# Channel shuffle: larger tiles, and each tile's copy halved over two engines

## The chip, the cores and the metric

The kernel runs on one core of a Trainium2 chip; the chip's other cores run nothing of it. The metric is the device time of one execution in microseconds (us). The *span* of a profile is the traced part of one execution; it is some 2 us shorter than the device time.

## The reference

The input has 256 float32 channels for each of 16 x 64 x 64 = 65,536 pixels. The channels are read as 8 groups of 32, and the two indices are swapped. Nothing is computed: 67.1 MB come in and 67.1 MB go out, in another order inside each pixel's 1 KB.

```python
x = x.reshape(batch, h, w, groups, channels_per_group)   # 16, 64, 64, 8, 32
x = x.transpose(0, 1, 2, 4, 3)
x = x.reshape(batch, h, w, c)
```

## The kernel before

A tile is 128 partitions x 16 pixels (16 KB a partition, 2 MB in all), and there are 32 of them. SyncE issues the loads, ScalarE issues the stores, and the swap of indices is one copy with a strided read. The copies go to GpSimd and VectorE in turn. There are five buffers for loaded tiles and five for tiles to be stored.

```python
_Q = 16; _IN_BUFS = 5; _OUT_BUFS = 5; _COPY_ENGINES = "gv"     # (shortened)
# ... pools in_pool and out_pool with that many buffers ...
for t in range(ntiles):                                        # 32
    in_tile = in_pool.tile([P, free], mybir.dt.float32)
    nc.sync.dma_start(out=in_tile, in_=x_t[t])
    out_tile = out_pool.tile([P, free], mybir.dt.float32)
    src = in_tile.rearrange("p (i g j) -> p i j g", g=G, j=CPG)
    dst = out_tile.rearrange("p (i j g) -> p i j g", j=CPG, g=G)
    do_copy(copy_engines[t % len(copy_engines)], dst, src)
    nc.scalar.dma_start(out=out_t[t], in_=out_tile)
```

## Time and profile before

| | before |
|---|---|
| device time, median | 318.0 us (317.92 to 318.02) |
| span of the profile | 316.3 us |
| VectorE / GpSimd busy | 20% / 36% of the span |
| DMA rate from 40 to 280 us | 431 GB/s, read plus written |

These lines are from the page of the kernel before. The row "DMA" gives the busy share of the 16 DMA engines in 40 equal slices of the span, in tenths; the row "GB/s" gives what they moved. The two lines that begin with L61 are the groups of copies: busy time and mean ns of one, then the idle time before them and what ended it.

```profile
span 316.3 us, 247 instructions
...
DMA  7999999999999999999999999999999999999997
GB/s 290 431 402 431 431 431 431 431 431 433 431 431 431 431 431 431 431 431 431 431 431 431 431 431 431 431 431 431 431 431 431 431 431 431 431 431 431 433 431 332
DMA packets 9216, 134.22 MB, mean 424 GB/s; under 512 B 1024, under 2 KB 1024, under 8 KB 1024
...
DMA 94%; DVE 1%; SPq 0%; issue 0%; DVEq 0%
DMA in_tile<-in_x_dram 94%; DVE out_tile L61 1%; SPq L65 0%; DVEq L61 0%
...
L61 POOL COPY out_tile<-in_tile 128x4096 f32<-128x4096 f32 x16 | 114.5, 7157 | 182.3 <-DMA in_tile<-in_x_dram 182.3
L61 DVE COPY out_tile<-in_tile 128x4096 f32<-128x4096 f32 x16 | 63.8, 3985 | 240.0 <-DMA in_tile<-in_x_dram 240.0
```

The DMA row is 9 nearly everywhere and the rate hardly moves. Both copy engines spend most of their time waiting for loads. The chain of waits, the two lines with 94% and 94%, consists of loads. In the trace's packet records, a data packet is one partition's row: 8,192 packets of 16,384 bytes, and 1,024 packets of 4 bytes that report completions to semaphores. Divided over the 16 DMA engines, that is 512 data packets and 64 semaphore packets each.

The table by stretches of the same trace (start:end in us, length, busy us of each engine with the number of instructions, TensorE's clock, DMA share, GB/s) shows where DMA is not saturated: only in the first and the last few us.

```profile
core 0: us, DVE busy (x) POOL busy (x), PEclk, DMA share, GB/s
0.00:40.00 40.00, 9.66 (x2) 18.02 (x7) 1.00 0.96 397
40.00:280.00 240.00, 46.34 (x12) 89.59 (x13) 1.00 1.01 431
280.00:312.00 32.00, 7.76 (x2) 7.11 (x1) 1.00 1.01 431
312.00:316.27 4.27, 0.00 (x0) 0.00 (x0) 1.00 0.58 249
```

Here 1.01 is no error of rounding. More than 16 packet records are open at times, so on one DMA engine the record of a packet must begin a little before the record of the packet before it ends.

### The profile page before, as it was taken

Reading aid. Unit: us, or ns where it says so; the run is one execution under the profiler, and the core shown is the slowest. Engines: PE = TensorE matmul, PEld = TensorE weight load, DVE = VectorE, ACT = ScalarE, POOL = GpSimd, SP = SyncE. Lnnn points to the kernel's source line nnn. Section 1 sums busy time; section 2 is a strip of 40 time slices with the busy share of each in tenths; the row PEclk is TensorE's granted clock in tenths of the full one; section 3 lists DMA queues with packets and bytes.
Section 4 is the critical chain, followed back from the end, with each engine's and each line's share of the span. In section 5 each row is a group of like instructions: output and inputs, shape, how many; then the busy total and the mean of one; then the engine's idle time right before and its main releaser. Section 6 shows DMA issues by size and latency. Waiting matters only on the chain.

```text
span 316.3 us, 247 instructions
## 1 busy us (share of the span) xinstructions
DVE 63.8 (20%) x16; POOL 114.7 (36%) x20
## 2 busy tenths in 40 slices
DVE  0344004040130402204021040310404004040040
POOL 0863350803508044080530806217062260713500
DMA  7999999999999999999999999999999999999997
GB/s 290 431 402 431 431 431 431 431 431 433 431 431 431 431 431 431 431 431 431 431 431 431 431 431 431 431 431 431 431 431 431 431 431 431 431 431 431 433 431 332
DMA packets 9216, 134.22 MB, mean 424 GB/s; under 512 B 1024, under 2 KB 1024, under 8 KB 1024
## 3 DMA queue, kind: packets, MB, share of 16 engines
q1 hardware_dynamic: 4608, 67.11, 50.0%
q10 hardware_dynamic: 4608, 67.11, 49.5%
HBM read 67.11 MB, written 67.11 MB: 424 GB/s over the span
## 4 chain that ended last, share of the span: by engine, by line
DMA 94%; DVE 1%; SPq 0%; issue 0%; DVEq 0%
DMA in_tile<-in_x_dram 94%; DVE out_tile L61 1%; SPq L65 0%; DVEq L61 0%
## 5 line engine op out<-in xcount | busy, mean ns | idle before, releaser
L61 POOL COPY out_tile<-in_tile 128x4096 f32<-128x4096 f32 x16 | 114.5, 7157 | 182.3 <-DMA in_tile<-in_x_dram 182.3
L61 DVE COPY out_tile<-in_tile 128x4096 f32<-128x4096 f32 x16 | 63.8, 3985 | 240.0 <-DMA in_tile<-in_x_dram 240.0
L90 POOL MEMSET const-float32-0.0<- 128x1 f32 x1 | 0.1, 99 | 0.2 <-issue 0.2
L90 POOL MEMSET const-bfloat16-1.0<- 128x1 bf16 x1 | 0.1, 103 | 0.0
L90 POOL MEMSET const-uint8-127<- 128x1 uint8 x1 | 0.1, 103 | 0.0
L90 POOL MEMSET const-float32-1.0<- 128x1 f32 x1 | 0.1, 99 | 0.0
## 6 DMA issues: line engine op xcount, KB each, us to landing
in_tile<-in_x_dram SPq DMA_DIRECT2D x32, 2048.0 KB, 38.8
out_dram<-out_tile ACTq DMA_DIRECT2D x32, 2048.0 KB, 25.3
```

The lines of the kernel that those rows point to most:

```text
L61: eng.tensor_copy(out=dst, in_=src)
L90: nc = _bacc.Bacc("TRN2", target_bir_lowering=False, num_devices=1)
```

## The change

Its intent is to move the same bytes in fewer, larger transfers, with the copy shortened by splitting each tile between VectorE and ScalarE, which leaves GpSimd free. There are 21 tiles of 24 KB a partition (3 MB) and a last one of 8 KB a partition, so that the last copy and store are short.

```diff
-_Q = 16
-_IN_BUFS = 5
-_OUT_BUFS = 5
-_COPY_ENGINES = "gv"
+_SIZES = [24] * 21 + [8]
+_IN_BUFS = 4
+_OUT_BUFS = 4
+_SHARES = (("vector", 1), ("scalar", 1))
 ... (row addressing for unequal tiles left out)
-    for t in range(ntiles):
-        ...
-        do_copy(copy_engines[t % len(copy_engines)], dst, src)
-        nc.scalar.dma_start(out=out_t[t], in_=out_tile)
+    for q in _SIZES:
+        in_tile = in_pool.tile([P, biggest * c], F32, name="in_tile")
+        nc.sync.dma_start(out=in_tile[:, : q * c], in_=rows(x_flat, first, q))
+        out_tile = out_pool.tile([P, biggest * c], F32, name="out_tile")
+        ... (for each engine of _SHARES, its columns:)
+                permute(engine, out_tile[:, cols], in_tile[:, cols])
+        nc.scalar.dma_start(out=rows(out_flat, first, q), in_=out_tile[:, : q * c])
+        first += P * q
```

More of the change, by code (lines that the diff above doesn't have):

```diff
@@ L2 @@
-import os
 from contextlib import ExitStack
@@ L8 @@
 from concourse._compat import with_exitstack
-_Q = int(os.environ.get("CS_Q", "16"))
-_IN_BUFS = int(os.environ.get("CS_IN_BUFS", "5"))
-_OUT_BUFS = int(os.environ.get("CS_OUT_BUFS", "5"))
-_COPY_ENGINES = os.environ.get("CS_COPY_ENGINES", "gv")
+F32 = mybir.dt.float32
+P = 128
+_SIZES = [24] * 21 + [8]
+_IN_BUFS = 4
+_OUT_BUFS = 4
+_SHARES = (("vector", 1), ("scalar", 1))
 @with_exitstack
@@ L29 @@
     CPG = c // G
-    assert G * CPG == c, (c, G)
-    P = nc.NUM_PARTITIONS
-    n_pix = b * h * w
-    assert n_pix % P == 0
-    q = _Q
-    pix_per_tile = P * q
-    ntiles = n_pix // pix_per_tile
-    assert ntiles * pix_per_tile == n_pix, (n_pix, pix_per_tile)
-    free = q * c
-    x_t = x.rearrange("b h w c -> (b h w c)").rearrange(
-        "(t p f) -> t p f", p=P, f=free
-    )
-    out_t = out.rearrange("b h w c -> (b h w c)").rearrange(
-        "(t p f) -> t p f", p=P, f=free
-    )
+    assert G * CPG == c
@@ L51 @@
+    assert sum(_SIZES) * P == b * h * w
+    biggest = max(_SIZES)
+    x_flat = x.rearrange("b h w c -> (b h w c)")
+    out_flat = out.rearrange("b h w c -> (b h w c)")
     in_pool = ctx.enter_context(tc.tile_pool(name="in_pool", bufs=_IN_BUFS))
     out_pool = ctx.enter_context(tc.tile_pool(name="out_pool", bufs=_OUT_BUFS))
-    eng_map = {"v": nc.vector, "g": nc.gpsimd, "s": nc.scalar}
-    copy_engines = [eng_map[ch] for ch in _COPY_ENGINES]
-    def do_copy(eng, dst, src):
-        if eng is nc.scalar:
-            eng.copy(out=dst, in_=src)
-        else:
-            eng.tensor_copy(out=dst, in_=src)
@@ L63, with rows @@
-    for t in range(ntiles):
-        in_tile = in_pool.tile([P, free], mybir.dt.float32)
-        nc.sync.dma_start(out=in_tile, in_=x_t[t])
-        out_tile = out_pool.tile([P, free], mybir.dt.float32)
-        src = in_tile.rearrange("p (i g j) -> p i j g", g=G, j=CPG)
-        dst = out_tile.rearrange("p (i j g) -> p i j g", j=CPG, g=G)
-        do_copy(copy_engines[t % len(copy_engines)], dst, src)
-        nc.scalar.dma_start(out=out_t[t], in_=out_tile)
+    def rows(flat, first, q):
+        return flat[first * c : (first + P * q) * c].rearrange("(p f) -> p f", p=P)
@@ new lines, in permute @@
+    def permute(engine, dst, src):
+        src = src.rearrange("p (i g j) -> p i j g", g=G, j=CPG)
+        dst = dst.rearrange("p (i j g) -> p i j g", j=CPG, g=G)
+        if engine == "scalar":
+            nc.scalar.copy(out=dst, in_=src)
+        else:
+            getattr(nc, engine).tensor_copy(out=dst, in_=src)
+    first = 0
+    for q in _SIZES:
+        in_tile = in_pool.tile([P, biggest * c], F32, name="in_tile")
+        nc.sync.dma_start(out=in_tile[:, : q * c], in_=rows(x_flat, first, q))
+        out_tile = out_pool.tile([P, biggest * c], F32, name="out_tile")
+        at, total = 0, sum(n for _, n in _SHARES)
+        for k, (engine, n) in enumerate(_SHARES):
+            last = k == len(_SHARES) - 1
+            upto = q if last else min(q, at + -(-q * n // total))
+            if upto > at:
+                cols = slice(at * c, upto * c)
+                permute(engine, out_tile[:, cols], in_tile[:, cols])
+            at = upto
+        nc.scalar.dma_start(out=rows(out_flat, first, q), in_=out_tile[:, : q * c])
+        first += P * q
```

## The prediction

> **What bounds the kernel now.** The 16 DMA engines, from end to end. The page's 40 slices show the DMA row at 9 (90% or more) in 38 of 40 and 431 GB/s in nearly all; the table by stretches gives a DMA share of 1.01 and 431 GB/s over 40 to 280 us. The queue table adds up to 99.5% of the span. VectorE is busy 20%, GpSimd 36%; both only wait for loads (240.0 and 182.3 us in the groups). The chain of waits is 94% DMA loads. In the trace's packet records nearly all 8192 data packets are 16384 bytes and last 611 ns; each of the 1024 semaphore packets lasts 9 ns. Per DMA engine that is 512 x 0.611 + 64 x 0.009 = 313.4 us: the whole span of 316.3 us less about 1.8 us before the first packet and 1.2 us after the last. The Trainium skill (DMA: Bandwidth & Descriptors, "Where 436 GB/s comes from") puts the fabric ceiling at 435.2 GB/s; the trace runs at 99% of it.
>
> **What the change does not touch.** The bytes: 67.1 MB in and 67.1 MB out.
>
> **What it changes, costed.**
> - The copy. A half tile is 3072 elements a partition: VectorE 3072/4096 x 3.87 us = 2.9 us (estimate from the steady copies). No ScalarE copy is in this trace; I guess 2.5 to 5 us. Both run at once, per tile period of 6.29 MB / 431 GB/s = 14.6 us, so neither engine comes near to binding. GpSimd's 114.7 us vanish. On the critical path: nothing.
> - Load depth. In the trace a load is issued when the fourth load before it lands (38.8 us to landing = four periods of 9.7 us). Afterwards it also waits for the copy out of its buffer: about 4 x 14.6 - 3 = 55 us to landing. The load queue stays full; stores also stay queued (about 25 us to landing). No starvation.
> - The start. The first load lands at about 10.9 us, not 8.5, but 12 MB of loads are queued by then, so DMA stays busy. The store backlog at the end (last load lands near 300 us, some 14 us of stores remain) hides the last copy as before; the small last tile therefore buys nothing.
> - Packets. 24 KB in place of 16 KB: 352 data and 44 semaphore packets per DMA engine in place of 512 and 64. Semaphores save 20 x 9 ns = 0.2 us. If a data packet has a fixed cost (611 ns against 602 ns at the ceiling of 435.2 GB/s leaves at most 9 ns; the same page, "Why small descriptors are slow", tells of a small fixed cost per packet), 160 fewer save up to 1.4 us. The trace cannot tell a fixed cost from a proportional one, so I take about half: 0.6 us.
>
> **Prediction.** 318.0 - 0.8 = 317.2 us, range 316.2 to 318.3. Chances: faster by over 2% 0.01, within 2% 0.98, slower by over 2% 0.01.
>
> **What would show each step right or wrong.** DMA row still at 9 and some 431 to 433 GB/s from start to end; 24 KB packets at 912 ns (fixed cost) or 916 ns (proportional); ScalarE and VectorE each under 40% busy, waiting for loads; the chain still over 90% DMA; loads about 55 us to landing; span about 315.5 us.
>
> **What would make it wrong.** Slices where the DMA share falls below 0.9: loads waiting for buffers with the queue empty, or stores held up on ScalarE's queue behind a copy that waits for a load. A ScalarE copy over 14 us, which would bind. Or the larger packets running at another rate, higher or lower, for a reason that the records of before don't show.

## The result

The time after is 317.73 us (317.58 to 317.88, 4 runs), against 318.01 us (317.92 to 318.13, 4 runs) for the kernel before. The ratio is 0.999, with a 95% interval from 0.9976 to 1.0005: the same. Ratios here are the mean time of one kernel's fast runs over that of the other's fast runs in the same rounds, so they are not quite the ratios of the medians quoted. Executions over 1.5% slower than the fastest of the same kernel are left out of the means.

The page of the kernel after, the lines that answer to those shown of before:

```profile
span 316.0 us, 236 instructions
...
DMA  8999999999999999999999999999999999999996
GB/s 302 439 395 426 426 445 432 420 442 439 417 439 445 417 436 442 426 426 445 426 423 445 439 414 442 442 417 439 442 421 432 442 420 432 442 429 429 421 446 291
DMA packets 6337, 134.23 MB, mean 425 GB/s; under 512 B 704, under 2 KB 704, under 8 KB 704
...
another core or an unknown queue 43%; DMA 32%; ACT 20%; ACTq 1%; issue 0%
DMA in_tile<-in_x_dram 32%; ACT out_tile L49 20%; ACTq L66 1%; ACTq L49 0%
...
L49 ACT COPY out_tile<-in_tile 128x3072 f32<-128x3072 f32 (+1 forms) x22 | 117.7, 5348 | 184.6 <-DMA in_tile<-in_x_dram 184.6
L51 DVE COPY out_tile<-in_tile 128x3072 f32<-128x3072 f32 (+1 forms) x22 | 65.3, 2968 | 238.3 <-DMA in_tile<-in_x_dram 238.3
...
in_tile<-in_x_dram SPq DMA_DIRECT2D x21, 3072.0 KB, 52.6
out_dram<-out_tile ACTq DMA_DIRECT2D x21, 3072.0 KB, 20.2
```

And the table by stretches of the kernel after:

```profile
40.00:280.00 240.00, 50.22 (x17) 89.29 (x17) 0.00 (x0) 1.00 1.00 432
280.00:312.00 32.00, 5.41 (x3) 10.89 (x3) 0.00 (x0) 1.00 0.99 426
312.00:315.97 3.97, 0.00 (x0) 0.00 (x0) 0.00 (x0) 1.00 0.44 188
```

The DMA row is as full as before. The rate in the middle stretch is 432 in place of 431 GB/s. The groups' mean mixes the small tile in; the groups kept apart by shape give 5.51 us for ScalarE's half of a 24 KB tile and 3.06 us for VectorE's. Both engines still wait for loads.

The chain of waits looks quite different: loads fell from 94% to 32%, ScalarE's copy appears with 20%, and 43% has no known releaser. That is no new bottleneck. With four buffers a load is issued when the copy frees its buffer, no longer when an earlier load lands. The waits of SyncE's queue show it; first before, then after:

```profile
SPq L65 <- DMA in_tile<-in_x_dram: 244.1, 27, 10.0
```

```profile
SPq L56 <- DVE out_tile L51: 184.6, 17, 12.0
...
SPq L56 <- ACT out_tile L49: 39.7, 17, 2.6
```

So the walk back from the last instruction now steps from load to copy to load. But the DMA engines had other loads and stores queued all the while, as the DMA row shows, and the time hardly changed. Two of the experiments below fit this, and show that the turn doesn't come from the halved copy: e4, the fastest kernel, copies in the old way with three buffers and has 34% loads in its chain; e2, with the halved copy and five buffers, has 87%.

One more thing is seen in the trace, and it matters in the experiments. ScalarE copies its halves and also issues the stores, one instruction after the other. From the third tile on its instructions come in the order copy, copy, store, store, although the kernel's text writes a store after each copy. So every second store stands behind the next tile's copy, and that copy waits for its load:

```profile
292.64 5.43 ACT L49 COPY out_tile<-in_tile 128x3072 f32<-128x3072 f32 x1 [9.11 <-DMA in_tile<-in_x_dram]
302.35 1.94 ACT L49 COPY out_tile<-in_tile 128x1024 f32<-128x1024 f32 x1 [4.29 <-DMA in_tile<-in_x_dram]
302.41 2.25 ACTq L66 DMA_DIRECT2D out_dram<-out_tile  x2
```

The tile copied from 292.64 us was ready at 298.07, but its store was issued at 302.41, just after the last copy had begun (the line with x2 merges this issue with that of the last tile). In all, 10 of the 22 stores of after were held in this way, for up to 9.3 us; in before, every store was issued within 0.03 us of its copy. With four buffers the DMA engines had enough other work: at 302.4 us, about 0.9 MB of earlier stores was still unfinished.

### The profile page after: what moved, and what is told of

It reads as the page before. It is cut to its first block, busy times and chain, and to the rows that moved or that the text cites. A ratio compares the mean times of both kernels' runs of the same rounds, so it can differ in the third digit from the quotient of the medians.

```text
span 316.0 us, 236 instructions
## 1 busy us (share of the span) xinstructions
DVE 65.3 (21%) x22; ACT 118.9 (38%) x23; POOL 0.2 (0%) x4
## 4 chain that ended last, share of the span: by engine, by line
another core or an unknown queue 43%; DMA 32%; ACT 20%; ACTq 1%; issue 0%
DMA in_tile<-in_x_dram 32%; ACT out_tile L49 20%; ACTq L66 1%; ACTq L49 0%
## 5 line engine op out<-in xcount | busy, mean ns | idle before, releaser
L49 ACT COPY out_tile<-in_tile 128x3072 f32<-128x3072 f32 (+1 forms) x22 | 117.7, 5348 | 184.6 <-DMA in_tile<-in_x_dram 184.6
L51 DVE COPY out_tile<-in_tile 128x3072 f32<-128x3072 f32 (+1 forms) x22 | 65.3, 2968 | 238.3 <-DMA in_tile<-in_x_dram 238.3
## 6 DMA issues: line engine op xcount, KB each, us to landing
in_tile<-in_x_dram SPq DMA_DIRECT2D x21, 3072.0 KB, 52.6
out_dram<-out_tile ACTq DMA_DIRECT2D x21, 3072.0 KB, 20.2
```

The lines of the kernel that those rows point to most:

```text
L49: nc.scalar.copy(out=dst, in_=src)
L51: getattr(nc, engine).tensor_copy(out=dst, in_=src)
```

## Where the gain in the steady part went

From the packet records one can work out three terms of a span. The first is the time that all 134.2 MB would take at the rate measured from 40 to 280 us. The second is what the start costs beyond that: 40 us less the time that the bytes moved up to 40 us need at that rate. The third is the same for the end, from 280 us on. They add up to the span. (One trace each; the sizes are KB a partition.)

| kernel | span, us | all bytes at the steady rate | lost at the start | lost at the end |
|---|---|---|---|---|
| before, 16 KB | 316.3 | 311.2 | 3.5 | 1.6 |
| after, 24 KB | 316.0 | 310.3 | 3.5 | 2.1 |

The change gained 0.87 us in the steady part, and lost 0.56 us at the end. The span is 0.3 us shorter, as is the time. Differences of some tenths between single traces need care: the spans of before scatter from 316.0 to 316.5 us. But the steady term repeats. It is 311.2 and 311.3 us in e1 and e2 below, which have 16 KB too, and 310.3 us in e8 and e12, which have 24 KB.

The steady part obeys a simple sum. From the number of packets served between 40 and 280 us, one can compute the time from one data packet to the next on one DMA engine: 607.8 ns for 16 KB and 909.1 ns for 24 KB, the semaphore packets included. The Trainium skill (DMA: Bandwidth & Descriptors, "Where 436 GB/s comes from") gives a ceiling of 435.2 GB/s, which is 27.2 bytes per ns for one of 16 engines. At that rate 16,384 bytes take 602.4 ns and 24,576 bytes take 903.5 ns. In both cases about 5.5 ns remain. A fixed cost of about 5.5 ns a packet was thus the theory to be tested (called F below). The records' own lengths, 611 and 912 ns, would give about 9 ns (called R), but they overlap, as the DMA share of 1.01 shows.

## The experiments

Runs e1 to e4, e5 to e8, e9 to e11, and e12 were four groups on three chips; each group shared its runs of the kernel before, which gave medians of 318.08, 318.05, 318.05 and 317.99 us.

### e1: no copy at all

```diff
-_IN_BUFS = 5
+_IN_BUFS = 10
-        do_copy(copy_engines[t % len(copy_engines)], dst, src)
-        nc.scalar.dma_start(out=out_t[t], in_=out_tile)
+        nc.scalar.dma_start(out=out_t[t], in_=in_tile)
```

> The kernel before without any copy (ten buffers of one pool, each tile stored as it was loaded; the result is wrong on purpose). Theory T1, the DMA engines bind from end to end and the copies are hidden: 318.0 us, as before, within 0.4. Rival T2, the copies or the engines they run on cost part of the time: at least 1 us under before.

It measured 318.69 us (318.46 to 318.92, 5 runs), ratio 1.0022 (1.0008 to 1.0036). Its output is wrong, which doesn't matter for the time. Taking away every copy saves nothing, so T2 falls. Nor do the copies slow the packets: their pace was 607.8 ns here as well. It is even 0.6 us slower, more than the 0.4 us that T1 allowed; its profiled span was 316.3 us, like that of before. Device time less span was 2.1 us in all five executions, against 1.8 us in before, so about half of the 0.6 us lies outside the profiled span. The cause stays open.

### e2: the halved copy alone

```diff
-_SIZES = [24] * 21 + [8]
-_IN_BUFS = 4
-_OUT_BUFS = 4
+_SIZES = [16] * 32
+_IN_BUFS = 5
+_OUT_BUFS = 5
```

> The new code with the old tile size and buffer counts (32 tiles of 16 KB a partition, five buffers): only the halved copy on VectorE and ScalarE changes. T1: 318.0 us within 0.3, so none of the 0.3 us gain belongs to the copy. T2, the gain comes from the copy: 317.7 us as after.

It measured 319.0 us (318.78 to 319.41, 5 runs), ratio 1.0031 (1.0019 to 1.0044). Neither number was met. The gain does not come from the halved copy, which cost about 0.9 us here. Its span was 317.0 us: 311.3 at the steady rate, 3.5 at the start, 2.2 at the end. So 0.6 of the 0.7 us lost in the span lies at the end, where 1.69 us passed after the last packet in place of 1.17 us. Nearly all of that is in one place: SyncE's first drain instruction after its last wait began 0.4 us later than in before, and took 0.12 us longer. Why is not known.

### e3, e4 and e5: other row lengths, the old copies

```diff
-_Q = 16;  _IN_BUFS = 5;   _OUT_BUFS = 5
+_Q = 8;   _IN_BUFS = 10;  _OUT_BUFS = 10      # e3
+_Q = 32;  _IN_BUFS = 3;   _OUT_BUFS = 3       # e4
+_Q = 4;   _IN_BUFS = 20;  _OUT_BUFS = 20      # e5
```

> The kernel before with 8 KB a partition (64 tiles, ten buffers): twice the packets. From the two traces, a 16 KB packet occupies its DMA engine for 607.8 ns from one to the next and a 24 KB one for 909.1 ns, so about 5.5 ns beyond the line rate, a fixed cost that includes the semaphore packets. Theory F with this cost: 512 more packets per engine x 5.5 ns = +2.8 us, 320.8 us. Rival R, the length of the packet records (9 ns a packet and 9 ns a semaphore packet): +5.0 us, 323.0 us. Rival P, no fixed cost: 318.0 us.

> The kernel before with 32 KB a partition (16 tiles, three buffers each): half the packets, whole-tile copies still on GpSimd and VectorE in turn. F: 256 fewer packets per engine x 5.5 ns = -1.4 us, 316.6 us. R: -2.5 us, 315.5 us. P: 318.0 us.

> The kernel before with 4 KB a partition (128 tiles, twenty buffers): four times the packets. F (5.5 ns a packet): 1536 more packets per engine, +8.4 us, 326.4 us. R (9 ns a packet and 9 ns a semaphore packet): +15.0 us, 333 us. P: 318.0 us.

| KB a partition | measured, us (range, runs) | ratio | F said | R said |
|---|---|---|---|---|
| 4 (e5) | 328.02 (327.76 to 328.29, 6) | 1.0315 | 326.4 | 333 |
| 8 (e3) | 322.12 (321.72 to 322.62, 4) | 1.0129 | 320.8 | 323.0 |
| 32 (e4) | 316.67 (316.52 to 317.10, 5) | 0.9961 | 316.6 | 315.5 |

P, no effect of the packets, falls. F meets 32 KB, and is 1.3 and 1.6 us short at 8 and 4 KB. The three terms say why:

| kernel | span, us | all bytes at the steady rate | lost at the start | lost at the end |
|---|---|---|---|---|
| e5, 4 KB | 326.2 | 319.9 | 3.6 | 2.7 |
| e3, 8 KB | 320.8 | 314.1 | 3.5 | 3.2 |
| e4, 32 KB | 315.3 | 309.8 | 3.7 | 1.7 |

In the steady part F holds for all: +8.7 us at 4 KB (8.4 expected), +2.9 at 8 KB (2.8), -1.4 at 32 KB (-1.4). From one packet to the next it is 156.2, 306.8 and 1210.1 ns, that is 5.6, 5.6 and 5.4 ns more than the bytes need at 27.2 bytes per ns. The page's ceiling is not even needed: a straight line through the five paces (4 to 32 KB) has a slope of 27.2 bytes per ns and leaves 5.6 ns, and no pace is off it by more than 0.11 ns. What these runs cannot tell is to what the fixed cost belongs. In each of them a transfer is eight data packets and one semaphore packet on each engine, so 5.5 ns a packet and some 44 ns a transfer would look alike. The rest is lost at the end, and differs from kernel to kernel by up to 1.6 us. The steady stretches of 4, 8 and 32 KB, in that order:

```profile
40.00:280.00 240.00, 52.60 (x48) 92.08 (x48) 1.00 1.03 420
```

```profile
40.00:280.00 240.00, 48.70 (x24) 89.85 (x25) 1.00 1.01 427
```

```profile
40.00:280.00 240.00, 45.13 (x6) 92.10 (x7) 1.00 1.00 433
```

The DMA share, the second-last figure of a line, falls from 1.03 to 1.00 while the rate rises from 420 to 433 GB/s. The more packets there are, the more records overlap. A DMA share of 1 does not mean that there is nothing to gain.

### e8: the small tile first

```diff
-_SIZES = [24] * 21 + [8]
+_SIZES = [8] + [24] * 21
```

> The new kernel with its small tile first instead of last. If the last copy is hidden under the stores still queued, the small last tile buys nothing: 317.7 us within 0.3. Rival, it shortens the tail: at least 1 us slower than after, since the last copy is then 5.4 us instead of 1.9 and the last store 3 MB instead of 1 MB.

It measured 317.34 us (317.27 to 317.70, 4 runs), ratio 0.9980 (0.9967 to 0.9994). That is 0.06 us below the range named for the first theory. The rival falls: with a full 24 KB tile last, nothing is lost. By the three terms, 3.5 us were lost at the start and 1.9 us at the end, no more than in after. The medians say 0.4 us faster than after, but the two intervals of the ratios overlap, so no more is claimed than that the small last tile buys nothing.

### e6 and e7: two buffers each

```diff
-_IN_BUFS = 4
-_OUT_BUFS = 4
+_IN_BUFS = 2
+_OUT_BUFS = 2
```

In e7 the sizes are `[48] * 10 + [32]` as well.

> The new kernel with two buffers for loads and two for stores in place of four. If a queue of DMA work never runs dry because loads and stores back each other up: 317.7 us within 0.5. Rival, the depth of four is needed: over 320 us, with slices where the DMA share falls below 0.9.

> The new kernel with tiles of 48 KB a partition (ten, and a last one of 32 KB), two buffers each: 176 packets per engine in place of 352. F: 176 x 5.5 ns = 1.0 us under after, 316.7 us, if nothing is lost at the ends. R: -1.7 us, 316.0 us. If the larger tiles lose at the start and at the end what they save per packet, as after seems to have done (0.87 us saved in the steady part, 0.3 us in the span): 317.7 us or more.

Both missed by far. e6 measured 325.9, 330.9 and four times 334.4 to 335.3 us. The profiled execution was the fastest, so the others count as slow ones beside it and there is no ratio; on one core this says only that its times scatter. e7 measured 335.91 us (335.86 to 336.83, 4 runs), ratio 1.0569. The halved number of packets was worth nothing beside what two buffers cost.

Stretches of e7: the early part, a later part, and a gap near the end.

```profile
40.00:130.00 90.00, 11.56 (x3) 26.78 (x3) 0.00 (x0) 1.00 1.00 375
140.00:200.00 60.00, 8.48 (x3) 18.29 (x3) 0.00 (x0) 1.00 1.00 432
302.00:308.00 6.00, 0.51 (x1) 0.55 (x1) 0.00 (x0) 1.00 0.13 57
```

Two different losses are seen. From 302 to 308 us the DMA engines were nearly idle (0.13): the last load had landed, and the last copy waited for a store to land and free its buffer. But there was work to do. The tile before the last, 6.3 MB, had been copied by 298.74 us; its store stood behind that last copy in ScalarE's order and was issued at 307.53 us. From 40 to 130 us, on the other hand, the DMA engines were busy throughout, at 375 GB/s in place of 432. There the packets themselves took longer: on average 43 ns per KB on the loads' queue and 44 on the stores' queue, in place of 37.8. What made them slow, and what ended it near 135 us, is not known. Of e6 only the fastest execution has a trace. It shows a weaker effect of the kind with 24 KB rows: from 40 to 280 us, at 428 GB/s, its load packets took 38.8 ns per KB, against 38.0 in after, and its store packets 38.0. So 48 KB rows are not needed for some slowing. Whether they made it larger, and what the other executions of e6 lost, is not known.

### e9 and e10: which of the two was short

```diff
 e9:                     e10:
 _IN_BUFS = 4            -_IN_BUFS = 4
-_OUT_BUFS = 4           +_IN_BUFS = 2
+_OUT_BUFS = 2            _OUT_BUFS = 4
```

> The new kernel with four buffers for loads and two for stores. Two and two were slow (335 us, 326 us in the profiled execution), and there both copy engines waited for stores to land. Theory O, the two store buffers are the shortage (a copy can't start until the store before the last has landed, so no store backlog forms, and loads stop while the copy waits): as slow as two and two, over 322 us. Rival I, the two load buffers are the shortage: 317.7 us within 0.7.

> The new kernel with two buffers for loads and four for stores. Theory O: 317.7 us within 0.7, with copies waiting for loads again. Rival I: over 322 us. If only both shortages together do harm, this run and the one with four and two are both near 318 us.

e9 measured 323.16 us (322.87 to 324.36, 4 runs), ratio 1.0169. e10 measured 322.59 us (318.88 to 323.44, 4 runs), ratio 1.0120; the execution of 318.88 us lost far less, and has no trace. Each shortage alone costs several us, so neither theory was the whole answer: O was right on e9, I on e10.

The waits of the copies, in e9 and then in e10 (who waits for whom: us in total, times, longest):

```profile
DVE out_tile L51 <- DMA out_dram<-out_tile: 230.2, 20, 16.0
ACT out_tile L49 <- DMA out_dram<-out_tile: 180.9, 20, 13.5
```

```profile
DVE out_tile L51 <- DMA in_tile<-in_x_dram: 241.8, 22, 13.8
ACT out_tile L49 <- DMA in_tile<-in_x_dram: 187.9, 22, 11.2
```

With two store buffers nearly every copy waits for a store; with two load buffers all wait for loads, as in after. Stretches near the end of e9, and at the start, in the middle and near the end of e10:

```profile
290.00:292.20 2.20, 0.00 (x0) 0.00 (x0) 0.00 (x0) 1.00 0.24 101
308.00:310.00 2.00, 1.10 (x1) 1.68 (x1) 0.00 (x0) 1.00 0.46 197
```

```profile
16.00:20.00 4.00, 1.93 (x1) 2.62 (x2) 0.00 (x0) 1.00 0.91 270
40.00:280.00 240.00, 48.43 (x16) 88.47 (x17) 0.00 (x0) 1.00 1.00 432
304.00:308.00 4.00, 1.09 (x1) 1.94 (x1) 0.00 (x0) 1.00 0.74 315
```

In its profiled execution e10 kept 432 GB/s in the middle, and lost its time at the ends: by the three terms 4.8 us at the start (3.5 in after) and 5.0 us at the end (2.1 in after). At 16 to 20 us both its buffers had been loaded and the first store had only just been issued: the third load was issued only at 16.71 us, when the first copy had freed a buffer. That loss belongs to the two load buffers.

Near the end it is the order of ScalarE's instructions again:

```profile
296.24 5.46 ACT L49 COPY out_tile<-in_tile 128x3072 f32<-128x3072 f32 x1 [9.08 <-DMA in_tile<-in_x_dram]
305.91 1.94 ACT L49 COPY out_tile<-in_tile 128x1024 f32<-128x1024 f32 x1 [4.21 <-DMA in_tile<-in_x_dram]
305.97 2.25 ACTq L66 DMA_DIRECT2D out_dram<-out_tile  x2
```

The tile copied from 296.24 us was ready at 301.70, but its store of 3 MB was issued at 305.97, behind the last copy, which waited for the last load. All but some 0.2 MB of the earlier stores had finished by then, so the DMA engines had run dry. In after the same store was held as long, with 0.9 MB still unfinished. Why e10 had less left at that moment is not known: over most of the run the lead, that is the bytes loaded less the bytes stored, was no smaller than in after (on average 7.8 MB from 60 to 280 us, against 7.6).

In e9 the loads were far ahead (a lead of 14 MB at 200 us), but each of the last copies had to wait until a store freed a buffer, and the store of the tile just finished was held behind such a copy. At 290 us the DMA engines ran dry while a tile ready at 289.44 was not issued until 292.30; at 308 us, while one ready at 306.46 was not issued until 308.38. By the three terms, about 4 of the 5.5 us that its span is longer than that of after were lost at the end (6.2 in place of 2.1 us), and 1.6 us in the middle, at 430 GB/s.

So the copies near the end stay hidden only while earlier stores keep the DMA engines busy. That finished tiles were held when the DMA engines ran dry is seen in the traces of e6, e7, e9 and e10. That the losses at the end would go if the stores were issued from an engine that doesn't copy is likely, but not shown: no run with two buffers did so.

### e11: a candidate

```diff
-_SIZES = [24] * 21 + [8]
-_IN_BUFS = 4
-_OUT_BUFS = 4
-_SHARES = (("vector", 1), ("scalar", 1))
+_SIZES = [8] + [32] * 15 + [24]
+_IN_BUFS = 3
+_OUT_BUFS = 3
+_SHARES = (("vector", 1),)
```

> A candidate for beating both: rows of 32 KB a partition (fifteen tiles, one of 8 KB first and one of 24 KB last), three buffers each, and VectorE alone copies (8 us a tile of a period of 19.4 us). Theory F with the copies hidden: 259 packets per engine in place of 512, -1.4 us against before: 316.6 us, as the 32 KB rows with two copy engines gave. If a single copy engine holds up the DMA engines: over 318 us.

It measured 316.78 us (316.54 to 318.85, 6 runs), ratio 0.9969 (0.9950 to 0.9988). Its groups of copies:

```profile
L51 DVE COPY out_tile<-in_tile 128x8192 f32<-128x8192 f32 x15 | 112.3, 7485 | 167.9 <-DMA in_tile<-in_x_dram 167.9
```

VectorE alone, busy 38% of the span, is enough. e11 equals e4 (316.67 us), which is the fastest kernel: 0.4% under before. Three buffers each are enough at 32 KB.

### e12: the new tiles with the old copies

```diff
-        ... (VectorE copies the first half of the columns, ScalarE the second)
+        permute("vector" if t % 2 else "gpsimd", out_tile[:, : q * c], in_tile[:, : q * c])
```

> The new kernel's tiles, order and buffers, but each tile copied whole, on GpSimd and VectorE in turn as in the kernel before: only the tile size changes. The halved copy alone came out 0.9 us slower than before (319.0 against 318.1 us), the new kernel 0.3 us faster. If the change is the sum of a gain by fewer packets (160 x 5.5 ns = 0.9 us) and a small cost of the copy's new form (0.6 to 0.9 us): 317.1 us here, within 0.3. If the two parts don't add up and the tile size gives only 0.3 us: 317.7 us.

It measured 317.56 us (317.44 to 317.67, 5 runs), ratio 0.9986 (0.9973 to 1.0000). The parts don't add up: e12 came out 0.4 us under before, much as after did, although e2 had put a cost on the halved copy. Its span of 315.8 us is 310.3 at the steady rate, 3.4 at the start and 2.1 at the end. It has the gain of after in the steady part, and the loss of after at the end, without any copy on ScalarE. So the loss at the end came with the new tiles and buffers, and doesn't need ScalarE's copies. After the last packet 1.17 us passed in before, 1.54 us in after and 1.42 us in e12. The instruction records show where: after the last landing, SyncE passes through five waits some 60 ns apart in after, e8 and e12, and through one in before, e1, e4 and e2. The four more waits are about 0.24 us, all that e12 has more. In after, VectorE's last instruction also ends 0.14 us after that of any other engine. The rest of the 0.56 us lost at the end, about 0.2 us, falls before the last packet ends and is not explained.

## Why the prediction was right, point by point

- **What bounds the kernel.** Right. The DMA row stayed full, and e1 showed that without any copy the time does not fall.
- **The copies are off the path.** Right. VectorE's half took 3.06 us (2.9 predicted). ScalarE's half took 5.51 us, above the guess of 2.5 to 5. Neither matters in a tile period of 14.6 us.
- **Load depth and the start.** Right in effect: 52.6 us to landing for loads (55 predicted) and 20.2 us for stores (25 predicted). The first copy began at 11.04 us (first load at 10.9 predicted). "No starvation" holds for four buffers; e9 and e10 show that it fails with two of either kind. One thing that the prediction named under "what would make it wrong" did happen: stores were held on ScalarE's queue behind a copy that waits for a load, 10 of 22. In after no gap of the DMA row shows for it, since other stores and loads were queued.
- **The small last tile buys nothing.** Right (e8).
- **Packets.** Right in mechanism. The records of 24 KB packets are 912 ns long, which the prediction had named as the sign of a fixed cost. Taken by the records, the saving would have been 1.4 us and 0.2 us. By the pace of packets it is 0.87 us in the steady part, data and semaphore packets together; the prediction's 0.6 + 0.2 us was close, for the poor reason of taking half. That was luck.
- **The sum.** The time was 317.73 us, inside the range of 316.2 to 318.3 but 0.5 us above 317.2. The range also held the time before, 318.0, so a change that did nothing would have met it too; the steady part and e1 say more for the argument than the time does. The mis-sized term is the end. The prediction took the ends as unchanged, with 1.2 us after the last packet; after has 1.54 us there, and in all loses 0.56 us more at the end. The span was 316.0 us, not 315.5.
- **The sign that failed.** "The chain still over 90% DMA" was wrong: loads fell to 32%. A load now waits for a copy to free its buffer, so the chain runs through copies while the DMA engines remain busy with other work. The prediction had the wait itself ("Afterwards it also waits for the copy out of its buffer"), but did not carry it over to the chain.

## What to carry to other kernels

When a kernel's transfers already fill the DMA engines, compare the pace of packets with the line rate before you touch the compute: here at most 1% was to be had, through longer rows, and splitting the copies or moving them to other engines could give nothing. Longer rows need buffers: here three a side were enough at 32 KB, and two of either kind cost several us at 24 KB, far more than the packets save. That cost was measured only where ScalarE both copies and issues the stores. Look at the order of instructions on such an engine: a store that stands behind a copy waits for all that the copy waits for, and the trace shows it as a store issued just after the next copy begins. Judge a changed chain of waits by the DMA row beside it: a chain that turns from loads to copies costs nothing while the queues stay full.

## What the Trainium skill lacked or had wrong

- DMA: Bandwidth & Descriptors, "Why small descriptors are slow", tells of a fixed overhead of about three cycles per packet, with a 256-byte example. Here rows of 4 to 32 KB show a fixed 5.4 to 5.6 ns a packet, semaphore packets included (6.1 ns in the trace of e11, at 32 KB). It is still worth 1.4 us of 318 between 16 and 32 KB.
- The same page's rule to batch to at least 1 MiB for at least 75% of peak ("Measured") rests on a table of transfer sizes, issued from GpSimd. With queues kept full, transfers of 0.5 MB (e5), issued from SyncE and ScalarE, moved 420 GB/s, 96% of the ceiling of 435.2. The rule does not say whether it holds for transfers that are queued behind others; in this run smaller transfers were enough.
- HBM Reference, "Specifications (TRN2)", says that a core streaming alone measures about 425 GB/s. Here loads and stores mixed reached 433 GB/s at 32 KB.
- ScalarE: Activation LUTs, "What ACT_TABLE_LOAD costs", gives 186 ns + 0.833 ns an element for an ACTIVATE with constant scale and bias, that is 2.7 us for 3,072 elements. ScalarE's copy here (COPY in the trace), whose read steps 128 bytes from element to element, took 5.51 us, and 1.94 us for the 1,024 elements of the small tile: about 1.74 ns an element. SBUF — State Buffer, "Door 1: The DMA port swizzle", says in its note on cachelines that stepping to a new 16-byte line costs extra, without a number for ScalarE; that this is the cause was not tested. VectorE took 3.06 us for the same number of elements.
- No page read tells of DMA packets that slow down on all engines with both queues full, as in e7 (375 in place of 432 GB/s for some 90 us).
